# Prompt attention: V and the probabilities turned by VectorE in 32x32 squares, and a head's output row joined to the next head's scores

## The chip, the cores and the metric

The kernel runs on one core of one Trainium2 chip. TensorE does the matrix products, VectorE (DVE in the profile), ScalarE (ACT) and GpSimd (POOL) the rest of the arithmetic, and SyncE (SP) issues most transfers. The metric is the device time of one execution in microseconds (us); the median of several runs counts.

## The reference

One layer of a decoder trunk, for a prompt of 256 positions and for 8 sample sequences of 4 new positions that share the weights. All 288 rows go through one combined input projection; from it come a gated short convolution (mixer A), a dilated sliding-window attention (mixer B) and two gates. Behind them stand two output products, a norm, a gated convolution FFN and a second norm. Everything is float32.

What is changed here lies in mixer B for the prompt. It has three head groups with window and dilation (128, 1), (512, 4), (2048, 16), four heads of dimension 128 in each:

```python
sc = jnp.einsum('nrbqhd,nrbkhd->nrbhqk', qb, kw).astype(jnp.float32) * ATT_SCALE - bias
sc = jnp.where(valid[None, None, :, None], sc, -jnp.inf)
m = jnp.max(sc, axis=-1, keepdims=True)
p = jnp.exp(sc - m)
den = jnp.sum(p, axis=-1, keepdims=True)
o = jnp.einsum('nrbhqk,nrbkhd->nrbqhd', p / den, vw.astype(jnp.float32))
lse = jnp.swapaxes((m + jnp.log(den))[..., 0], 3, 4)
...
wg = jax.nn.softmax(jnp.stack(lses), axis=0)
yb = jnp.einsum('gnth,gnthd->nthd', wg, jnp.stack(outs)).reshape(n, t, ATT_OUT).astype(x.dtype)
```

Head j of the three groups is merged with weights that follow the softmax denominators. That equals one softmax over the keys of all three groups together, and the kernel computes it so: for one head j, one row of scores over group 0's keys and groups 1 and 2's keys of the same residue class, one exponential, one sum, one product with V.

## The kernel before

**Products.** Activations are kept transposed: features on the 128 partitions, 288 tokens along the columns. Each weight block (128 output features by up to 2048 input features) is loaded by SyncE into one of three buffers `wst` and split in two float32r parts, a half block of eight 128x128 tiles at a time: ScalarE rounds it to `whi`, VectorE subtracts to get `wlo` (`split`, L232). There are four buffers for each part. `mms` (L226, L227, L228) then issues three matmuls per tile (high x high, high weight x low activation, low weight x high activation), so a product of 16 tiles is 48 matmuls into one of six PSUM buffers `acc`. A half block can be refilled once TensorE has finished with what was in its buffers four half blocks before.

**Stages.** Queries of all heads come first. Then for each of the four heads j there are six products: K and V of the three groups. Behind these begins the attention of the prompt for head j, `prompt_attention`. It is a generator, which `prompt_step` moves on by one step behind each following product, so that its instructions fall into the next head's products (for the last head, into the products of the convolution stage that follows). A second, independent chain of steps (`sample_steps`) treats the sample group meanwhile: it multiplies tiles of the cache on ScalarE and VectorE (L478, L483) and reduces them with a transposing reduction on VectorE (L485).

**The order of the work.** A tile scheduler decides the order of each engine's instructions from the recorded program. What is held by hand: `behind(i, before)` orders one instruction behind another on its engine, and `in_a_row` does so for a list. A row of small matmuls is put behind the last matmul of a product (`last_mm`), so a row stands whole between two products.

**The attention of one head, before.** (1) GpSimd copies K and V of groups 1 and 2 into four classes by position (`k_cls`, `v_cls`, L379). (2) The scores' row on TensorE: two matmuls for group 0 (L384), and 32 of 32 rows each for the classes (L391), into two PSUM buffers `att`. (3) VectorE adds the distance penalties (L398, L404) and takes the maximum (L407, L408), ScalarE the exponential with its sum (L409), VectorE divides (L410, L411). Two blocks of 128 queries have 192 and 384 columns of probabilities. (4) Two products later a second row: six transposes of V (L418) and five of the probabilities (L423), 128x128 each, by TensorE against the identity. ScalarE copies the results out of PSUM in four instructions (L420 and L427). (5) One product later the third row, the output: six matmuls (L431, L432, L435), which sum V times probabilities over both kinds of keys, into another `att` buffer. ScalarE copies it to `oT` in token order (L441), and a split into `ybh`, `ybl` follows.

Of the kernel before, what the change touches and what calls it, by code (L numbers as in the profile page):

```python
# [18 lines left out]
P = 128  # L19
D = 2048  # L20
KD = D // P
SEQ = 256
NB, NT = 8, 4
NS = NB * NT
T = SEQ + NS
# [11 lines left out]
NG, NH = 3, 4  # L37
# [10 lines left out]
NM = NG * P  # L48
NC = 4
# [30 lines left out]
SQ = 32  # L80
# [18 lines left out]
def layer_kernel(ctx: ExitStack, tc: tile.TileContext, ins, outs):  # L99
    nc = tc.nc  # L100
    pe, dve, act, pool, sp = nc.tensor, nc.vector, nc.scalar, nc.gpsimd, nc.sync
# [4 lines left out]
    ps = ctx.enter_context(tc.tile_pool(name="ps", bufs=6, space=PSUM))  # L106
# [3 lines left out]
    def nm(s):  # L110
        uid[0] += 1
        return f"{s}_{uid[0]}"

    def sb(pl, shape, tag, dt=F32, bufs=None):
        return pl.tile(shape, dt, tag=tag, name=nm(tag), bufs=bufs)
# [4 lines left out]
    def h2(ap):  # L120
        return ap.rearrange("p (h a) -> p h a", h=2)

    def h3(ap):
        return ap.rearrange("p k (h a) -> p k h a", h=2)
# [5 lines left out]
    def att(cols=512):  # L130
        return sb(ps, [P, cols], "att", bufs=2)

    def f32(ap):
        return ap.bitcast(F32)
# [9 lines left out]
    def behind(i, after):  # L144

        tc.add_manual_dep(i.ins, after.ins.name, no_sync, reason="pace")
# [7 lines left out]
    w_split = []  # L154
# [40 lines left out]
    last_mm = [None]  # L195
# [35 lines left out]
    def split(hi, lo, src):  # L231
        return act.copy(hi, src), dve.tensor_tensor(lo, src, f32(hi), ALU.subtract)  # L232
# [29 lines left out]
    def first_w(lo, b, k0, n):  # L262
        k, h = slice(k0, k0 + n), slice(k0 % HK, k0 % HK + n)
        if b < 2:
            return (two_lo if lo else two_hi)[:, b, k]
        if b < 4 and not (lo and b == 3):
            return one[2 if lo else b - 2][:, k]
        return half[0 if b == 3 else 1 + lo][k0 // HK][:, h]

    raw, sp_row = [], []  # L270
    for n, (k0, nk) in enumerate(FIRST):
        k = slice(k0, k0 + nk)
# [4 lines left out]
    for n, (k0, nk) in enumerate(FIRST):  # L277
        k = slice(k0, k0 + nk)
        x_k = xs[:, k].rearrange("p k (a h) -> p k h a", h=2)
        act_row.append(act.copy(xh[:, k, :, :H], x_k))  # L280
        for b in range(1, N_FIRST):
            if b == 1:
                out, src = two_hi[:, :, k], raw[n][:, :2]
            else:
                out, src = first_w(False, b, k0, nk), raw[n][:, b]
# [33 lines left out]
    pa = sb(big, [P, KD * T], "yal")  # L319

    m_dist = [pa[:, :NM], pa[:, NM : 3 * NM]]
    v_cls = pa[:, 3 * NM : 3 * NM + 2 * 2 * P].rearrange("p (c k) -> p c k", c=NC)
    q_0 = pa[:, 3 * NM + 4 * P : 3 * NM + 6 * P].rearrange("p (b k) -> p b k", b=2)
    k_cls = pa[:, 3 * NM + 6 * P : 3 * NM + 10 * P].rearrange("p (c k) -> p c k", c=NC)
    pa_at = [3 * NM + 10 * P]

    def pa_take(n):
        pa_at[0] += n
        return pa[:, pa_at[0] - n : pa_at[0]]

    v = pa_take(2 * NG * P).rearrange("p (b d) -> p b d", d=P)
    s_two = [pa_take((b + 2) * P) for b in range(2)]
    xs_flat = xs.rearrange("p k t -> p (k t)")
    q_all = xs_flat[:, : NH * NG * T].rearrange("p (j g t) -> p j g t", j=NH, g=NG)
    sT_two = [xs_flat[:, NH * NG * T + 2 * b * P : NH * NG * T + (5 * b + 2 * (1 - b)) * P] for b in range(2)]
    sT_old = xs_flat[:, NH * NG * T : NH * NG * T + 4 * P].rearrange("p (b k) -> p b k", b=2)[:, :, :P]
    sT_cls = xs_flat[:, NH * NG * T : NH * NG * T + 6 * P].rearrange("p (b k) -> p b k", b=2)[:, :, P : 2 * P]
    oT = pa_take(2 * P)
    prm = sb(big, [P, R_W], "prm")
    ident = cst[:, C_ID : C_ID + P]  # L340

    ybh = sb(big, [P, NH, T], "ybh", F32R)
    ybl = sb(big, [P, NH, T], "ybl", F32R)
# [23 lines left out]
    def in_a_row(row):  # L367

        for before, i in zip(row, row[1:]):
            behind(i, before)  # L370

    def prompt_attention(j, qT, kT, vT):


        q5 = h3(qT)[:, :, :, :P].rearrange("p g r (b u c) -> p g b r c u", b=2, c=2)
        k_b, v_b = (t.rearrange("p c (b g u) -> p g c b u", b=2, g=2) for t in (k_cls, v_cls))
        for dst, src in ((k_b, kT), (v_b, vT)):
            for g in range(1, NG):
                pool.tensor_copy(dst[:, g - 1], src[:, g, :SEQ].rearrange("p (b u c) -> p c b u", b=2, c=NC))  # L379
        s3 = [att((b + 1) * P + (b + 1) * 2 * SQ) for b in range(2)]  # L380
        row = [last_mm[0]]
        for b in range(2):
            n = (b + 1) * P
            row.append(pe.matmul(s3[b][:, :n], q_0[:, b], kT[:, 0, :n], start=True, stop=True))  # L384
        for b in range(2):
            by_class = s3[b][:, (b + 1) * P :].rearrange("p (b g u) -> p g b u", g=2, u=SQ)
            for g in range(1, NG):
                for r in range(2):
                    for c in range(2):
                        at = slice(SQ * (2 * r + c), SQ * (2 * r + c + 1))  # L390
                        row.append(pe.matmul(  # L391
                            by_class[at, g - 1], q5[:, g, b, r, c], k_b[:, g - 1, 2 * c + r, : b + 1], start=True, stop=True
                        ))
        in_a_row(row)
        s = [s_two[b][:, : (b + 1) * (P + 2 * SQ)] for b in range(2)]
        for b in range(2):
            n = (b + 1) * P
            dve.scalar_tensor_tensor(  # L398
                s[b][:, :n], m_dist[b][:, :n], -SLOPE[0][j] / SCALE, s3[b][:, :n], ALU.mult, ALU.add
            )  # L400
            dst, src = (t[:, n:].rearrange("p (b g u) -> p g b u", g=2, u=SQ) for t in (s[b], s3[b]))
            for g in range(1, NG):
                m = m_dist[b][:, g * n : (g + 1) * n].rearrange("p (b u c) -> p b u c", u=SQ, c=NC)[:, :, :, 0]
                dve.scalar_tensor_tensor(dst[:, g - 1], m, -SLOPE[g][j] / SCALE, src[:, g - 1], ALU.mult, ALU.add)  # L404
        for b in range(2):
            st = sb(wk, [P, 4], "st", bufs=4)
            dve.reduce_max(st[:, 0:1], s[b], AX.X)  # L407
            dve.tensor_scalar_mul(st[:, 1:2], st[:, 0:1], -SCALE)  # L408
            act.activation(s[b], s[b], AF.Exp, bias=st[:, 1:2], scale=SCALE, accum_out=st[:, 2:3])  # L409
            dve.reciprocal(st[:, 3:4], st[:, 2:3])  # L410
            dve.tensor_scalar_mul(s[b], s[b], st[:, 3:4])  # L411
        yield 2
        pv = [att(NG * P) for _ in range(2)]
        row = [last_mm[0]]
        for n in range(2 * NG):
            out = pv[n // NG][:, n % NG * P : (n % NG + 1) * P]
            src = vT[:, 0, n * P : (n + 1) * P] if n < 2 else v_cls[:, n - 2]
            row.append(pe.transpose(out, src, ident))  # L418
        for n in range(2):
            act.copy(v[:, n * NG : (n + 1) * NG], pv[n].rearrange("p (b d) -> p b d", d=P))  # L420
        pt = [sb(ps, [P, (b + 2) * P], "acc") for b in range(2)]
        in_a_row(row + [
            pe.transpose(pt[b][:, c * P : (c + 1) * P], s_two[b][:, c * P : (c + 1) * P], ident)  # L423
            for b in range(2) for c in range(b + 2)
        ])
        for sT, t in zip(sT_two, pt):
            act.copy(sT, t)  # L427
        yield 1
        po = att(2 * P)
        row = [last_mm[0]]  # L430
        row.append(pe.matmul(h2(po), v[:, 0], sT_old, start=True, stop=False))  # L431
        row.append(pe.matmul(po[:, P:], v[:, 1], sT_two[1][:, P : 2 * P], start=False, stop=False))  # L432
        for c in range(NC):
            at = slice(c * SQ, (c + 1) * SQ)
            row.append(pe.matmul(  # L435
                h2(po)[:, :, at], v[:, 2 + 2 * (c % 2) + c // 2], sT_cls[:, :, at], start=False, stop=c == NC - 1
            ))
        in_a_row(row)
        o_b = oT.rearrange("p (r b u c) -> p b r c u", r=2, b=2, c=2)
        for b in range(2):  # L440
            act.copy(o_b[:, b], po[:, b * P : (b + 1) * P].rearrange("p (r c u) -> p r c u", r=2, c=2))  # L441
        split(h2(ybh[:, j])[:, :, :P], h2(ybl[:, j])[:, :, :P], oT.rearrange("p (h a) -> p h a", h=2))

    bmask = cst[:, C_BM : C_BM + MASK]

# [179 lines left out]
    for j in range(NH):  # L627
        kT, vT = (kv[:, j % 2, c] for c in range(2))
# [58 lines left out]
    for i in range(KD):  # L687
        ph = product(x)
        h = sb(wk, [P, T], "h", bufs=2)
        act.copy(h2(h), ph)  # L690
        pc = product(x)
        u = sb(wk, [P, UW + 2], "u", bufs=2)
# [216 lines left out]
    for part, nf in enumerate(THIRDS):  # L909
        gh = sb(big, [P, KD, T], "yah", F32R)  # L910
        gl = sb(big, [P, KD, T], "yal", F32R)
        for k in range(nf):
            pa = product(x_gb if part == 0 else x)
            u = sb(wk, [P, UW + 2], "u", bufs=2)
            up, us = conv_in(u[:, :UW], R_SF + f * 2 * NB)
            if part == 0:
                pa, b1 = normed(pa)
# [230 lines left out]
```

## Time and profile before

| What | Value |
|---|---|
| Median of 3 runs | 1723.63 us (1723.46 to 1723.65) |
| Profiled execution, its own time | 1723.19 us |
| Its span (first to last instruction) | 1721.4 us |
| Granted TensorE clock, mean | 0.998 |
| TensorE busy | 1709.2 us, 99% of the span |
| VectorE, ScalarE, GpSimd busy | 1122.3 (65%), 879.1 (51%), 275.0 us (16%) |
| Scores' rows of the four heads begin at | 115.19, 154.58, 193.98, 233.38 us |
| Rows of transposes begin at | 128.29, 167.70, 207.09, 246.50 us |
| Output rows begin at | 135.38, 174.78, 214.18, 253.59 us |

A matmul's duration in the profile is the time from its start to its modelled end. Matmuls overlap, so the time that one takes from TensorE is read from the starts of neighbours. A time in square brackets behind an instruction of another engine is the idle time just before it, with what ended it. All four heads lie between 70 and 260 us of the span; after that stage the kernel's work is not touched by the change.

### The profile page before, as it was taken

The numbers are of one execution on the slowest core, as the hardware profiler recorded it, in microseconds if no ns is written. First come the engines' busy times: TensorE is split into PE (matmuls) and PEld (weight loads), VectorE is DVE, ScalarE is ACT, GpSimd is POOL, SyncE is SP. The second block draws the span as 40 slices with busy tenths as digits, with TensorE's granted clock in tenths as the row PEclk, the third lists the DMA queues.
The fourth block names the chain that finished last, engine by engine and source line by source line (L and its number), as shares of the span: only waits on it lengthen the run. The fifth ranks groups of instructions, "written<-read, shape, count | busy, mean of one in ns | idle before, by whom it ended". The sixth has DMA issues, their size and how long they took to land.

```text
span 1721.4 us, 33808 instructions
## 1 busy us (share of the span) xinstructions
PE 1709.2 (99%) x14132; PEld 1703.5 (99%) x14132; DVE 1122.3 (65%) x1448; ACT 879.1 (51%) x1432; POOL 275.0 (16%) x431
## 2 busy tenths in 40 slices
PE   9999999999999999999999999999999999999997
PEld 9999999999999999999999999999999999999997
DVE  6457677775777765455788878855556554555575
ACT  5446555554555554444545655543455543344455
POOL 0011110000000000001454323300111100011165
PEclk9999999999999999999999999999999999999999
DMA  8766666665767776688876666667766766766662
GB/s 293 289 259 250 236 222 248 238 243 204 263 245 252 294 289 245 245 306 302 301 258 253 245 253 257 249 247 262 275 247 258 254 245 257 281 245 254 244 219 108
DMA packets 60824, 436.17 MB, mean 253 GB/s; under 512 B 7744, under 2 KB 13632, under 8 KB 21056
## 3 DMA queue, kind: packets, MB, share of 16 engines
q1 hardware_dynamic: 59376, 430.33, 68.0%
q10 hardware_dynamic: 1296, 3.69, 0.6%
q8 instruction: 110, 1.80, 0.4%
q14 instruction: 42, 0.34, 0.1%
HBM read 427.53 MB, written 94.53 MB: 303 GB/s over the span
## 4 chain that ended last, share of the span: by engine, by line
PE 99%; DMA 0%; DVE 0%; ACT 0%; SPq 0%; issue 0%; ACTq 0%; DVEq 0%
PE acc L226 32%; PE acc L227 32%; PE acc L228 32%; PE acc L311 2%; DMA wst<-in_w_in 0%; PE att L514 0%; DVE dd L861 0%; PE att L435 0%; PE att L418 0%; PE att L384 0%; PE acc L423 0%; ACT yah L868 0%; PE att L391 0%; PE att L544 0%; PE att L431 0%; DVE yah L859 0%
## 5 line engine op out<-in xcount | busy, mean ns | idle before, releaser
L232 DVE TENSOR_TENSOR wlo<-wst,whi 128x1024 fp32r<-128x1024 f32 (+1 forms) x574 | 703.1, 1225 | 464.5 <-ACT whi L232 460.5
L232 ACT CAST whi<-wst 128x1024 fp32r<-128x1024 f32 (+1 forms) x574 | 586.2, 1022 | 761.4 <-PE acc L227 688.9
L226 PE MATMUL acc<-xh,whi 128*128 128x288 f32 (+1 forms) x3184 | 909.2, 286 | 0.0
L227 PE MATMUL acc<-xl,whi 128*128 128x288 f32 (+1 forms) x3184 | 907.7, 285 | 0.0
L228 PE MATMUL acc<-xh,wlo 128*128 128x288 f32 (+1 forms) x3184 | 907.6, 285 | 0.0
L226 PEld LDWEIGHTS acc<-xh,whi 128*128 128x128 f32 x3184 | 599.1, 188 | 1.4 <-issue 0.8
L228 PEld LDWEIGHTS acc<-xh,wlo 128*128 128x128 f32 x3184 | 599.1, 188 | 0.0
L227 PEld LDWEIGHTS acc<-xl,whi 128*128 128x128 f32 x3184 | 599.0, 188 | 0.0
L228 PE MATMUL acc<-yah,wlo 128*128 128x288 f32 x1216 | 347.7, 286 | 0.0
L227 PE MATMUL acc<-yal,whi 128*128 128x288 f32 x1216 | 347.7, 286 | 0.0
L226 PE MATMUL acc<-yah,whi 128*128 128x288 f32 x1216 | 347.6, 286 | 0.0
L228 PEld LDWEIGHTS acc<-yah,wlo 128*128 128x128 f32 x1216 | 229.8, 189 | 0.0
L227 PEld LDWEIGHTS acc<-yal,whi 128*128 128x128 f32 x1216 | 229.8, 189 | 0.0
L226 PEld LDWEIGHTS acc<-yah,whi 128*128 128x128 f32 x1216 | 229.7, 189 | 0.0
L668 POOL COPY qk_s<-u 128x2 f32<-128x2 f32 x44 | 36.4, 828 | 562.7 <-ACT u L922 441.6
L485 DVE TRANSPOSE_TENSOR_REDUCE sw<-cache 128x32 f32<-128x1024 f32 x64 | 79.7, 1245 | 5.2 <-ACT cache L478 1.1
L656 DVE SCALAR_TENSOR_TENSOR cy<-u,prm,cy 128x304 f32<-128x304 f32 x120 | 70.7, 589 | 3.5 <-ACT cy L654 0.7
L727 POOL TENSOR_TENSOR ya<-ya,dd 128x288 f32<-128x288 f32 x16 | 13.8, 859 | 294.4 <-DVE ya L726 288.8
L478 ACT ACTIVATE cache<-cache,qk_s 128x128 f32<-128x128 f32 x128 | 43.2, 392 | 0.0
L232 ACT CAST yah<-ya 128x288 fp32r<-128x288 f32 x76 | 32.5, 428 | 20.5 <-POOL ya L727 8.2
L478 ACT ACTIVATE cache<-cache,dd 128x128 f32<-128x128 f32 x128 | 42.1, 390 | 0.0
L679 DVE TENSOR_TENSOR ya<-cy,acc 128x256 f32<-128x256 f32 x88 | 23.3, 304 | 25.6 <-PE acc L228 25.6
(219 smaller groups left out, 1015.4 us busy)
## 6 DMA issues: line engine op xcount, KB each, us to landing
wst<-in_w_in SPq DMA_DIRECT2D x111, 1024.0 KB, 4.9
wst<-in_w_up SPq DMA_DIRECT2D x88, 1024.0 KB, 4.9
wst<-in_w_down SPq DMA_DIRECT2D x32, 1024.0 KB, 4.9
cache<-in_ck SPq DMA_DIRECT2D x18, 1024.0 KB, 6.5
cache<-in_cv SPq DMA_DIRECT2D x18, 1024.0 KB, 6.2
wst<-in_w_a SPq DMA_DIRECT2D x16, 1024.0 KB, 4.9
wst<-in_w_out SPq DMA_DIRECT2D x16, 1024.0 KB, 5.3
wst<-in_w_down SPq DMA_DIRECT2D x16, 768.0 KB, 4.4
```

The source lines that it names most:

```text
L226: pe.matmul(out, hi[:, c, :], xh_k, start=k == 0, stop=False)
L227: pe.matmul(out, hi[:, c, :], xl_k, start=False, stop=False)
L228: last_mm[0] = pe.matmul(out, lo[:, c, :], xh_k, start=False, stop=k == nk - 1)
L232: return act.copy(hi, src), dve.tensor_tensor(lo, src, f32(hi), ALU.subtract)
L311: i = pe.matmul(o[b], first_w(term == 2, b, k, 1)[:, 0], xk, start=k == 0 and term == 0, stop=k == KD - 1 and term == 2)
L478: i = act.activation(e_t, e_t, AF.Copy, scale=w[:, g + 1, j, b * NT + t : b * NT + t + 1])
L485: dve.tensor_reduce(parts[:, g, :, j, b * NT : (b + 1) * NT].rearrange("p k j t -> p j t k"), c[:, 2 * half * cols : (2 * half + 2) * cols ...
L656: dve.scalar_tensor_tensor(y, u[:, i : i + YW], prm[:, w0 + i : w0 + i + 1], y, ALU.mult, ALU.add)
L668: pool.tensor_copy(dst[:, 0:2], u[:, SEQ : SEQ + 2])
L679: dve.tensor_tensor(a, b, c, ALU.mult)
L727: pool.tensor_tensor(m, m, ma[:, i], ALU.add)
```

## The change

Steps (1) to (3) stay. Step (4) leaves TensorE:

- VectorE turns V and the probabilities in 32x32 squares, each square in its place: V of group 0 (256 columns) from `vT` into a new buffer `v_sq`; V's classes (512 columns, which GpSimd now writes into `v_sq`) in place; and all five blocks of probabilities (640 columns, now in one buffer `s_blk`) in place.
- A turned square of rows 32i and columns 32k still has to go to rows 32k and columns 32i. That is done by copies of one pair (i, k) for all blocks at once: 16 copies of 32 partitions by 6 x 32 for V, on ScalarE, into `v`; 16 copies of 32 partitions by 5 x 32 for the probabilities, on VectorE, into `sT_blk`. They are issued in parts: five of V's in the first step behind the scores, then with each of three products four (the last time three) of V's and six (the last time four) of the probabilities', and each is ordered behind the last weight split of its engine.

Step (5) is a function `output`, kept in `pending`: for heads 0 to 2 its six matmuls become the first part of the next head's scores' row, six products after the head's own scores. Its PSUM buffer is one of `acc` instead of `att`. For the last head the output row stands alone, six products after that head's scores, in the convolution stage.

```diff
-    v_cls = pa[:, 3 * NM : 3 * NM + 2 * 2 * P].rearrange("p (c k) -> p c k", c=NC)
...
+    v, v_sq, q_0, k_cls = (pa_blocks(n) for n in (2 * NG, 2 * NG, 2, NC))
+    v_cls = v_sq[:, 2:]
+    s_blk = pa_blocks(5)
+    s_two = [s_blk[:, 2 * b : 2 + 3 * b].rearrange("p b k -> p (b k)") for b in range(2)]
...
+    sT_blk = xs_flat[:, NH * NG * T : NH * NG * T + 5 * P].rearrange("p (b k) -> p b k", b=5)
...
+    pending = []
+
+    def output(j):
+
+        po = sb(ps, [P, 2 * P], "acc")
+        row = [pe.matmul(h2(po), v[:, 0], sT_old, start=True, stop=False)]
+        row.append(pe.matmul(po[:, P:], v[:, 1], sT_blk[:, 3], start=False, stop=False))
+        for c in range(NC):
+            at = slice(c * SQ, (c + 1) * SQ)
+            row.append(pe.matmul(
+                h2(po)[:, :, at], v[:, 2 + 2 * (c % 2) + c // 2], sT_cls[:, :, at], start=False, stop=c == NC - 1
+            ))
...
+        return row
+
     def prompt_attention(j, qT, kT, vT):
...
-        row = [last_mm[0]]
+        row = [last_mm[0]] + (pending.pop()() if pending else [])
...
-        yield 2
-        pv = [att(NG * P) for _ in range(2)]
-        row = [last_mm[0]]
-        for n in range(2 * NG):
-            out = pv[n // NG][:, n % NG * P : (n % NG + 1) * P]
-            src = vT[:, 0, n * P : (n + 1) * P] if n < 2 else v_cls[:, n - 2]
-            row.append(pe.transpose(out, src, ident))
-        for n in range(2):
-            act.copy(v[:, n * NG : (n + 1) * NG], pv[n].rearrange("p (b d) -> p b d", d=P))
-        pt = [sb(ps, [P, (b + 2) * P], "acc") for b in range(2)]
-        in_a_row(row + [
-            pe.transpose(pt[b][:, c * P : (c + 1) * P], s_two[b][:, c * P : (c + 1) * P], ident)
-            for b in range(2) for c in range(b + 2)
-        ])
-        for sT, t in zip(sT_two, pt):
-            act.copy(sT, t)
         yield 1
...
+        dve.transpose(v_sq[:, :2].rearrange("p b k -> p (b k)"), vT[:, 0, :SEQ])
+        v_c = v_cls.rearrange("p c k -> p (c k)")
+        dve.transpose(v_c, v_c)
+        s_all = s_blk.rearrange("p b k -> p (b k)")
+        v_moves, s_moves = ([(n, (n + r) % 4) for r in range(4) for n in range(4)] for _ in range(2))
+
+        def move(eng, dst, src, n, split_n):
+            for _ in range(n):
+                if moves[dst is v]:
+                    i, k = moves[dst is v].pop()
+                    at, to = slice(i * SQ, (i + 1) * SQ), slice(k * SQ, (k + 1) * SQ)
+                    behind((act.copy if eng is act else dve.tensor_copy)(dst[to, :, at], src[at, :, to]), w_split[split_n])
+
+        moves = s_moves, v_moves
+        move(act, v, v_sq, 5, 0)
+        yield 1
+        dve.transpose(s_all, s_all)
+        for n in range(3):
+            move(act, v, v_sq, 4, 0)
+            move(dve, sT_blk, s_blk, 6, 1)
+            yield 1
+        pending.append(partial(output, j))
+        if j == NH - 1:
+            yield 1
+            in_a_row([last_mm[0]] + pending.pop()())
```

In the changed program TensorE's instructions stand in the same order as before but for these rows, and SyncE's queue is the same instruction for instruction. On GpSimd only the order of a few copies for a head's first queries and classes changes.

More of the change, by code (lines that the diff above doesn't have):

```diff
@@ L321, in layer_kernel @@
     m_dist = [pa[:, :NM], pa[:, NM : 3 * NM]]
-    v_cls = pa[:, 3 * NM : 3 * NM + 2 * 2 * P].rearrange("p (c k) -> p c k", c=NC)
-    q_0 = pa[:, 3 * NM + 4 * P : 3 * NM + 6 * P].rearrange("p (b k) -> p b k", b=2)
-    k_cls = pa[:, 3 * NM + 6 * P : 3 * NM + 10 * P].rearrange("p (c k) -> p c k", c=NC)
-    pa_at = [3 * NM + 10 * P]
+    pa_at = [3 * NM]
     def pa_take(n):
@@ L329, in pa_take, with pa_blocks @@
         return pa[:, pa_at[0] - n : pa_at[0]]
-    v = pa_take(2 * NG * P).rearrange("p (b d) -> p b d", d=P)
-    s_two = [pa_take((b + 2) * P) for b in range(2)]
+    def pa_blocks(n):
+        return pa_take(n * P).rearrange("p (b k) -> p b k", b=n)
+    v, v_sq, q_0, k_cls = (pa_blocks(n) for n in (2 * NG, 2 * NG, 2, NC))
+    v_cls = v_sq[:, 2:]
+    s_blk = pa_blocks(5)
+    s_two = [s_blk[:, 2 * b : 2 + 3 * b].rearrange("p b k -> p (b k)") for b in range(2)]
     xs_flat = xs.rearrange("p k t -> p (k t)")
     q_all = xs_flat[:, : NH * NG * T].rearrange("p (j g t) -> p j g t", j=NH, g=NG)
-    sT_two = [xs_flat[:, NH * NG * T + 2 * b * P : NH * NG * T + (5 * b + 2 * (1 - b)) * P] for b in range(2)]
+    sT_blk = xs_flat[:, NH * NG * T : NH * NG * T + 5 * P].rearrange("p (b k) -> p b k", b=5)
     sT_old = xs_flat[:, NH * NG * T : NH * NG * T + 4 * P].rearrange("p (b k) -> p b k", b=2)[:, :, :P]
@@ L370, in in_a_row @@
             behind(i, before)
+    pending = []
[8 more added lines that the diff above has]
+            ))
+        o_b = oT.rearrange("p (r b u c) -> p b r c u", r=2, b=2, c=2)
+        for b in range(2):
+            act.copy(o_b[:, b], po[:, b * P : (b + 1) * P].rearrange("p (r c u) -> p r c u", r=2, c=2))
+        split(h2(ybh[:, j])[:, :, :P], h2(ybl[:, j])[:, :, :P], oT.rearrange("p (h a) -> p h a", h=2))
+        return row
     def prompt_attention(j, qT, kT, vT):
@@ L421, in prompt_attention @@
-        pt = [sb(ps, [P, (b + 2) * P], "acc") for b in range(2)]
-        in_a_row(row + [
-            pe.transpose(pt[b][:, c * P : (c + 1) * P], s_two[b][:, c * P : (c + 1) * P], ident)
-            for b in range(2) for c in range(b + 2)
-        ])
-        for sT, t in zip(sT_two, pt):
-            act.copy(sT, t)
-        yield 1
[L429 to L442, printed above, removed]
+        yield 1
```

## The prediction

> **What bounds the kernel now.** I read the page first: its first part (busy time) and fourth part (the chain that ended last), then TensorE's own list of waits, because a chain that is all TensorE can still hide starved stretches.
>
> ```profile
> PE 1709.2 (99%) x14132; PEld 1703.5 (99%) x14132; DVE 1122.3 (65%) x1448; ACT 879.1 (51%) x1432; POOL 275.0 (16%) x431
> ...
> PE 99%; DMA 0%; DVE 0%; ACT 0%; SPq 0%; issue 0%; ACTq 0%; DVEq 0%
> ```
> ```profile
> PE acc L311 <- ACT yal L289: 1.6, 2, 1.1
> PE acc L244 <- DVE cy L241: 1.2, 1, 1.2
> PE acc L841 <- DVE dd L861: 0.3, 1, 0.3
> PE acc L846 <- DVE h L833: 0.3, 1, 0.3
> ```
>
> Columns of the second view: who waits, for whom; total us, times, longest. These are all of TensorE's waits: start and end of the kernel, none in the attention stage. So an instruction taken off TensorE's queue between about 115 and 255 us shortens the kernel by its pitch (start to next start), not by its duration, as long as TensorE's inputs stay early. The prediction has two halves: how much pitch goes, and whether the inputs stay early.
>
> **What leaves TensorE: the transposes.** Each head has a row of 11 (six for V, L418; five for the probabilities, L423) between two products. First and last head in the timeline (start us, busy us, then the instruction and its count):
>
> ```profile
> 128.17 0.28 PE L228 MATMUL acc<-xh,wlo 128*128 128x288 f32 x1
> 128.29 0.38 PE L418 MATMUL att<-cst,dd 128*128 128x128 f32 x2
> 128.51 0.60 PE L418 MATMUL att<-cst,yal 128*128 128x128 f32 x4
> 128.95 0.71 PE L423 MATMUL acc<-cst,yal 128*128 128x128 f32 x5
> 129.41 0.37 PE L226 MATMUL acc<-xh,whi 128*128 128x288 f32 x1
> 129.62 0.29 PE L227 MATMUL acc<-xl,whi 128*128 128x288 f32 x1
> ...
> 246.50 0.38 PE L418 MATMUL att<-cst,dd 128*128 128x128 f32 x2
> ...
> 247.62 0.37 PE L226 MATMUL acc<-xh,whi 128*128 128x288 f32 x1
> 247.82 0.29 PE L227 MATMUL acc<-xl,whi 128*128 128x288 f32 x1
> ```
>
> Product matmuls start 0.12 us apart (128.17, 128.29). From the first transpose to the second product matmul behind the row is 129.62 - 128.29 = 1.33 us; one product pitch of 0.12 would be there anyway, so the row costs 1.21 us, of which 0.09 is the seam: the first product matmul behind it starts 0.21 before its successor instead of 0.12. The last head gives 1.32 - 0.12 = 1.20. Four heads: 4 x 1.205 = 4.82 us. Without transposes the seam goes too, so all of it counts.
>
> Within the row, 129.41 - 128.29 = 1.12 us for 11 is 0.10 us per transpose, although one alone lasts about 0.27 (two overlapped take 0.38, less one spacing). The Trainium skill, TensorE: Matmul & The Clock Gate, Part 4, gives about 275 ns for a transpose inside a kernel. That is this trace's duration, not its spacing; counted by it the sum would be 44 x 0.275 = 12.1 us by estimate, and this is a rival below.
>
> **What moves on TensorE: the output row.** It keeps its six matmuls per head, but for heads 0 to 2 stands directly ahead of the next head's scores:
>
> ```profile
> 135.38 0.59 PE L431 MATMUL att<-yah,yal 128*128 128x256 f32 x2
> ...
> 136.84 0.37 PE L226 MATMUL acc<-xh,whi 128*128 128x288 f32 x1
> 137.05 0.29 PE L227 MATMUL acc<-xl,whi 128*128 128x288 f32 x1
> ...
> 154.58 0.82 PE L384 MATMUL att<-dd,yal 128*128 128x128 f32 x4
> 155.32 0.56 PE L391 MATMUL att<-yal,yah 128*32 128x32 f32 x32
> 155.82 0.39 PE L226 MATMUL acc<-xh,whi 128*128 128x288 f32 x1
> 156.04 0.29 PE L227 MATMUL acc<-xl,whi 128*128 128x288 f32 x1
> ```
>
> The row takes 1.46 us and has the same exit seam, 0.21 - 0.12 = 0.09. Joined, three of these go: at most 0.27. The new joint between output and scores isn't in this trace; a change of shape inside a row costs something of the order of the exit seam, so the gain lies between 0 and 0.27. I take 0.2, nearer the measured seam. **Sum on TensorE:** 4.82 + 0.2 = 5.0 us.
>
> **What the other engines get.** Per head VectorE gains three square transposes over 256, 512 and 640 columns, and 16 copies of 32 partitions by 5 x 32 for the probabilities. ScalarE gains 16 copies of 32 by 6 x 32 for V, and loses the four evacuations of the transposes. GpSimd and SyncE keep their instructions; no DMA is added or moved in its queue. These rows bound the prices (the first is a line's own statistics, min/median/max ns):
>
> ```profile
> L287 DVE CAST cache<-wst x2: 222/224/226, 5.1 to 6.7; 128x128 fp32r<-128x128 f32 x2
> ```
> ```profile
> 155.73 0.29 DVE L398 SCALAR_TENSOR_TENSOR yal<-yal,att 128x128 f32<-128x128 f32 x1 [1.71 <-PE att L391]
> 155.93 0.32 DVE L404 SCALAR_TENSOR_TENSOR yal<-yal,att 128x32 f32<-128x32 f32 x2
> 156.18 1.21 DVE L232 TENSOR_TENSOR wlo<-wst,whi 128x1024 fp32r<-128x1024 f32 x1
> 157.31 0.75 DVE L483 TENSOR_TENSOR cache<-cache,qk_s 128x512 f32<-128x512 f32 x1
> 157.98 0.41 DVE L398 SCALAR_TENSOR_TENSOR yal<-yal,att 128x256 f32<-128x256 f32 x1
> 158.31 0.43 DVE L404 SCALAR_TENSOR_TENSOR yal<-yal,att 128x64 f32<-128x64 f32 x2
> ...
> 158.93 1.23 DVE L485 TRANSPOSE_TENSOR_REDUCE sw<-cache 128x32 f32<-128x1024 f32 x1
> 160.09 0.50 DVE L407 TENSOR_REDUCE st<-yal 128x1 f32<-128x384 f32 x1
> ...
> 161.95 0.32 DVE L411 TENSOR_SCALAR yal<-yal,st 128x192 f32<-128x192 f32 x1
> ```
> ```profile
> 170.20 0.84 ACT L420 COPY yal<-att 128x384 f32<-128x384 f32 x2
> 170.93 0.76 ACT L427 COPY yah<-acc 128x256 f32<-128x256 f32 x2
> ```
>
> A copy of 160 columns lies between the cast of 128 columns (0.22) and the scaling of 192 (0.32). I take 0.28; 16 make 4.5 us. Bounds: 0.12 (half the pair of 32-column instructions at 155.93, overlapped) and 0.75 (512 columns). The square transpose has its nearest row in the transposing reduction: 1.23 us for 1024 columns, pro rata 0.31, 0.61 and 0.77 for 256, 512 and 640. With a little fixed time each I take 0.4, 0.7 and 0.8, 1.9 per head; bounds 1.7 (pro rata) and 3.7 (1.23 each). VectorE: +6.4 us per head. ScalarE: 16 copies of 192 columns at 0.3 to 0.38 (the 256-column copy) are about 5.1 us, less 0.84 + 0.76: +3.5 us.
>
> All of this I cost at nothing, and the cover is the lead of the weight split. Each half block of weights is rounded by ScalarE (whi) and subtracted by VectorE (wlo) ahead of its product:
>
> ```profile
> 182.29 1.04 ACT L232 CAST whi<-wst 128x1024 fp32r<-128x1024 f32 x1 [1.90 <-PE acc L227]
> 185.23 1.05 ACT L232 CAST whi<-wst 128x1024 fp32r<-128x1024 f32 x1 [0.42 <-PE acc L227]
> ```
> ```profile
> 183.37 1.22 DVE L232 TENSOR_TENSOR wlo<-wst,whi 128x1024 fp32r<-128x1024 f32 x1 [1.72 <-ACT whi L232]
> ```
>
> TensorE frees a half block every 185.23 - 182.29 = 2.94 us; with four buffers it comes to the refilled one three half blocks later, 8.8 us after the release. The split is done 183.37 + 1.22 - 182.29 = 2.3 us after it: 6.5 us to spare. The whole gain hangs on whether the attention work eats these 6.5 us.
>
> ```profile
> 154.60:178.20 23.60, 23.60 (x221) 23.12 (x220) 17.39 (x28) 15.32 (x34) 3.90 (x5) 1.00 0.58 217
> ```
>
> This stretch (columns: length; busy of PE, PEld, DVE, ACT, POOL; granted clock, DMA share, GB/s) is the four products behind head 1's scores, where the new work falls. VectorE is busy 17.39 of 23.6 us; with 6.4 more it is full. So I walk its queue in the changed program's order, times from the start of the joined row:
>
> Scores end at 1.46 + 1.15 = 2.6 (155.73 - 154.58 = 1.15). Six bias additions, a transposing reduction, the earlier head's split and a maximum reach 5.6; V's transpose to 6.3; the rest of the statistics and one wlo to 8.1. ScalarE meanwhile does V's first five copies, which wait for that transpose, and stand ahead of both exponentials: these end at 9.5 and the next whi at 10.6, released at 8.7. VectorE scales, turns the probabilities (10.9), then wlo (12.1), a cache product, six copies, a reduction, and the wlo that ends at 16.8: TensorE needs it at 20.4, 3.6 to spare. The wlo behind the second six copies ends at 22.6 against 26.3, 3.7 to spare; behind the last four and the next head's first transpose, 26.3 against 32.2, 5.9 to spare. Then the queue drains (the next product's stretch is light). So the lead falls to 3.6 us and TensorE doesn't wait. Head 3 has two convolution additions in the stretch, and I find about 4 us there.
>
> Other waits. V's transpose waits for GpSimd's class copies:
>
> ```profile
> 157.46 1.11 POOL L379 COPY yal<-dd 128x256 f32<-128x256 f32 x1
> ```
>
> This ends 158.57 - 154.58 = 4.0 us into the row; VectorE comes to it at 5.6. The output row needs the last copies: they are issued two products ahead of it (over 10 us). Loads of raw weights follow the late wlo by its lateness, at most 3 to 4 us; a load is due 2.5 products (14.7 us) after the release that the wlo before it followed, which needs 2.3 us, the lateness and the landing:
>
> ```profile
> wst<-in_w_in SPq DMA_DIRECT2D x111, 1024.0 KB, 4.9
> ```
>
> That leaves 14.7 - 2.3 - 4.9 = 7.5, above the lateness.
>
> **Against which time.** The profiled execution took 1723.19 us (span 1721.4 and 1.8 around it), 0.44 below the median 1723.63. Less 5.0: 1718.2, or 1718.6 on the median's basis. I predict 1718.5.
>
> **Rivals.** *VectorE starves TensorE (slower).* Place: the first products behind each head's scores. With 16 copies at x us instead of 0.28, the spares above are used up at 0.28 + 3.7/12 = 0.59. A head then loses 16 (x - 0.59), and the gain of 1.25 per head is gone at x = 0.67. At 0.75, the 512-column row, each loses 2.6: 1718.5 + 10.2 = 1728.7. For it: VectorE has no reserve there, and every copy moves to other partitions. Against: five times fewer columns per copy would have to cost as much as 512.
> The pair of 32-column instructions at 155.93 overlaps (0.32 for two). The Trainium skill, VectorE: DVE Perf Modes, section Two Vector instructions with no wait between them, says that an instruction whose 32-partition quadrant differs from the one before is held until that has finished; the 16 copies alternate quadrants, so by it they don't overlap. By estimate that keeps them at 0.28 or more apart, which the walk assumes; no run here shows it yet.
>
> *Late in places.* One or two heads, most likely head 3, wait 1 to 4 us: 1719.5 to 1722.5. For it: a lead of under 4 us by a hand walk. Against: it is still a whole half block.
>
> *The saving counts by duration.* 44 x 0.27 = 11.9 us: 1711.7. Against it, the row of 11 begins and ends within 1.33 us.
>
> *No change.* Something else ends at the same time, 1723.6. Against: the chain and TensorE's empty wait list.
>
> **How the numbers follow.** Forecast 0.84 (own range 1717.6 to 1719.4: seam 0 to 0.27, the two bases, and some tenths); late in places 0.05; starved 0.06; by duration 0.02; no change 0.03. The range 1717.4 to 1720.4 holds the forecast and the milder part of the late case, some 0.86. A change of this kernel under 0.2% (3.4 us) can't be told from none. Faster: 0.84 + 0.02 + 0.03 of the late case = 0.89; same: 0.02 + 0.03 = 0.05; slower 0.06.
>
> **What would show it.** Right: no TensorE transposes until the sample group's own; the output row directly ahead of the next scores and about 2.7 us with them; TensorE's waits still empty in 115 to 275 us; ScalarE's and VectorE's small copies near 0.3 us each; wlo instructions up to 4 us later against their products. Wrong: idle time of TensorE put down to wlo (VectorE) or whi (ScalarE) there, copies above 0.55 us, or a square transpose well above a microsecond.

## The result and the profile after

| | Before | After |
|---|---|---|
| Median of 9 runs each, us | 1723.52 (1723.27 to 1723.95) | 1718.73 (1718.47 to 1719.67) |
| Profiled execution, us | 1723.19 | 1718.68 |
| Its span, us | 1721.4 | 1716.9 |
| Granted TensorE clock, mean | 0.998 | 0.999 |
| TensorE busy, us | 1709.2 | 1705.5 |
| VectorE, ScalarE busy, us | 1122.3, 879.1 | 1143.8, 895.4 |

The kernel is faster: the ratio after to before is 0.9972, with an interval of 0.9964 to 0.9981. The medians differ by 4.79 us.

The page of the changed kernel, its busy times and its chain; then the list of all that TensorE waits for:

```profile
PE 1705.5 (99%) x14088; PEld 1700.3 (99%) x14088; DVE 1143.8 (67%) x1524; ACT 895.4 (52%) x1480; POOL 280.3 (16%) x431
...
PE 99%; DVE 0%; ACT 0%; DMA 0%; ACTq 0%; issue 0%; DVEq 0%
```
```profile
PE acc L244 <- DVE cy L241: 1.2, 1, 1.2
PE acc L311 <- ACT yal L289: 0.9, 1, 0.9
PE acc L854 <- DVE dd L874: 0.3, 1, 0.3
PE acc L859 <- DVE h L846: 0.3, 1, 0.3
```

44 matmuls are gone (14132 to 14088), VectorE has 21.5 us and ScalarE 16.3 us more work, and the chain is TensorE's as before. The list of waits has no `wlo` and no `whi`: in the attention stage TensorE still waits for nothing.

TensorE's timeline (start us, busy us, then the instruction and its count) shows where the scores of head 0 begin, and the row of head 1 as it is now, the output of head 0 (from L379 on) and then the scores (from L404 on):

```profile
115.56 0.82 PE L404 MATMUL att<-dd,yal 128*128 128x128 f32 x4
...
152.21 0.59 PE L379 MATMUL acc<-yah,yal 128*128 128x256 f32 x2
...
153.70 0.87 PE L404 MATMUL att<-dd,yal 128*128 128x128 f32 x4
...
155.00 0.39 PE L226 MATMUL acc<-xh,whi 128*128 128x288 f32 x1
155.22 0.29 PE L227 MATMUL acc<-xl,whi 128*128 128x288 f32 x1
```

From the row's start to the second product matmul behind it is 155.22 - 152.21 = 3.01 us. Nothing is left of the row of transposes. To the first product matmul the joined row takes 155.00 - 152.21 = 2.79 us; the two rows before, read to the same point, take 1.46 + 1.24 = 2.70, which is the 2.7 that were forecast; the 0.09 more is the seam, which comes back at the joint (see the experiments). The span is 4.5 us shorter rather than 4.8 because head 0's scores begin 0.37 us later than before (115.56 against 115.19), ahead of all that the change touches.

What the change does in its stage can be read free of that: from head 0's first score to the first matmul of the sample group's own row behind the stage. These are its lines, before and after:

```profile
372.90 0.25 PE L535 MATMUL att<-qk_s 128*32 128x32 f32 x5
```
```profile
368.52 0.22 PE L548 MATMUL att<-qk_s 128*32 128x32 f32 x2
```

The stretch takes 372.90 - 115.19 = 257.71 us before and 368.52 - 115.56 = 252.96 us after, so 4.75 us less. It is called the stage below, and in one trace against another it shows differences that the spread of the medians hides.

The new instructions, each as the statistics of its line (min/median/max ns, from when to when):

```profile
L433 DVE STREAM_TRANSPOSE yal<-dd x4: 390/404/433, 93.3 to 216.6; 128x256 f32<-128x256 f32 x4
L435 DVE STREAM_TRANSPOSE yal<-yal x4: 665/696/701, 121.1 to 234.4; 128x512 f32<-128x512 f32 x4
L449 DVE STREAM_TRANSPOSE yal<-yal x4: 845/846/846, 128.4 to 239.2; 128x640 f32<-128x640 f32 x4
L444 ACT COPY yal<-yal x64: 347/349/353, 121.8 to 252.3; 32x192 f32<-32x192 f32 x64
L444 DVE COPY yah<-yal x64: 245/250/625, 130.3 to 254.2; 32x160 f32<-32x160 f32 x64
```

The three square transposes were taken at 0.4, 0.7 and 0.8 us, and have 0.404, 0.696 and 0.846. The copies of 160 columns were taken at 0.28 us and have 0.250.

VectorE's queue in head 1, the stretch that the prediction walked by hand (start us, busy us, line, count):

```profile
165.43 1.57 DVE L444 COPY yah<-yal 32x160 f32<-32x160 f32 x6
167.03 1.25 DVE L498 TRANSPOSE_TENSOR_REDUCE sw<-cache 128x32 f32<-128x1024 f32 x1
168.20 2.32 DVE L232 TENSOR_TENSOR wlo<-wst,whi 128x1024 fp32r<-128x1024 f32 x2
...
171.15 1.57 DVE L444 COPY yah<-yal 32x160 f32<-32x160 f32 x6
...
173.92 2.32 DVE L232 TENSOR_TENSOR wlo<-wst,whi 128x1024 fp32r<-128x1024 f32 x2
```

Six copies take 1.57 us and the last of them 0.25, so they start 0.264 apart, a little more than one lasts. A `wlo` takes about 1.18 us here. The first one behind the first six copies so ends at 169.38, which is 17.2 us after the row's start (16.8 in the prediction), and the first behind the second six at 175.10, 22.9 us after it (22.6).

### The profile page after: what moved, and what is told of

It reads as the page before. It is cut to its first block, busy times and chain, and to the rows that moved or that the text cites. A ratio compares the mean times of both kernels' runs of the same rounds, so it can differ in the third digit from the quotient of the medians.

```text
span 1716.9 us, 33841 instructions
## 1 busy us (share of the span) xinstructions
PE 1705.5 (99%) x14088; PEld 1700.3 (99%) x14088; DVE 1143.8 (67%) x1524; ACT 895.4 (52%) x1480; POOL 280.3 (16%) x431
## 4 chain that ended last, share of the span: by engine, by line
PE 99%; DVE 0%; ACT 0%; DMA 0%; ACTq 0%; issue 0%; DVEq 0%
PE acc L226 32%; PE acc L227 32%; PE acc L228 32%; PE acc L311 2%; DMA wst<-in_w_in 0%; PE att L527 0%; DVE dd L874 0%; PE acc L383 0%; PE att L404 0%; ACT yah L881 0%; PE att L411 0%; PE att L557 0%; PE acc L379 0%; DVE yah L872 0%; PE att L784 0%; PE acc L380 0%
## 5 line engine op out<-in xcount | busy, mean ns | idle before, releaser
L232 ACT CAST yah<-ya 128x288 fp32r<-128x288 f32 x76 | 32.5, 428 | 20.3 <-DVE ya L697 8.1
```

## The experiments

The theory under test (A): TensorE is the bound, the transposes cost it their spacing, and the new work of VectorE and ScalarE is hidden by the lead of the weight split. The rivals: the saving goes by the transposes' duration; the join carries a part of the gain; the new work costs something that the waits don't show (E in the expectations). All runs that follow are set against runs of the kernel before on the same chip: median 1723.85 us (18 runs) for the joined row, the squares, the doubled transposes and the copies three times; 1723.96 us (17 runs) for the others.

### The joined row without the squares

The kernel before, with its transposes on TensorE; only the output row is joined to the next head's scores. The diff leaves out the function `output`, which is that of the change.

```diff
...
-        row = [last_mm[0]]
+        row = [last_mm[0]] + (pending.pop()() if pending else [])
...
+        pending.append(partial(output, j))
+        if j == NH - 1:
+            yield 3
+            in_a_row([last_mm[0]] + pending.pop()())
```

> The kernel before with one part of the change: the output row joins the next head's scores (last head: alone), the 44 transposes stay on TensorE. Theory A (the joint costs as much as the seam it saves, read from the rows of the trace after): 1723.5 us, joined rows of 3.01 us to the second product matmul. Prediction's term (0.2 us saved, at most 0.27): 1723.3 us. Rival B (the joining carries the gain, the transposes were hidden): 1718.7 us.

Measured: 1723.68 us (1723.04 to 1724.43), ratio 1.0000 (0.9991 to 1.0009). Its timeline, TensorE, head 1's joined row:

```profile
153.21 0.59 PE L377 MATMUL acc<-yah,yal 128*128 128x256 f32 x2
...
154.70 0.87 PE L402 MATMUL att<-dd,yal 128*128 128x128 f32 x4
...
156.00 0.39 PE L226 MATMUL acc<-xh,whi 128*128 128x288 f32 x1
156.22 0.29 PE L227 MATMUL acc<-xl,whi 128*128 128x288 f32 x1
```

It is again 156.22 - 153.21 = 3.01 us long. The median moves by nothing that can be measured, but its interval is wide enough to hide the 0.2 us that were forecast. The stage is sharper: 373.06 - 115.36 = 257.70 us, against 257.71 before. Joining alone brings nothing.

### The squares without the joined row

The changed kernel, but each head's output row stands alone, a product ahead of the next head's scores.

```diff
-        pending.append(partial(output, j))
-        if j == NH - 1:
-            yield 1
-            in_a_row([last_mm[0]] + pending.pop()())
+        in_a_row([last_mm[0]] + output(j))
...
-        row = [last_mm[0]] + (pending.pop()() if pending else [])
+        row = [last_mm[0]]
```

> The changed kernel with the output row standing alone one product ahead of the next scores: the squares without the joining. Theory A (all of the gain is the pitch of the 44 transposes, 4 x 1.20 us): 1718.7 us. Prediction's terms: 1718.9 us. Rival B (the joining carries the gain): 1723.5 us. A wait of TensorE for the last copies of V or of the probabilities, which now have one product less of time, would add up to a few us and stand in TensorE's waits at the output row.

Measured: 1718.54 us (1718.32 to 1718.93), ratio 0.9969 (0.9956 to 0.9981): the whole gain, without the join. Its stage takes 368.37 - 115.48 = 252.89 us, 4.82 less than before. Its timeline, TensorE, the output row of head 0 and the scores' row of head 1:

```profile
146.24 0.59 PE L379 MATMUL acc<-yah,yal 128*128 128x256 f32 x2
...
147.71 0.37 PE L226 MATMUL acc<-xh,whi 128*128 128x288 f32 x1
147.91 0.29 PE L227 MATMUL acc<-xl,whi 128*128 128x288 f32 x1
...
153.67 0.82 PE L404 MATMUL att<-dd,yal 128*128 128x128 f32 x4
...
155.14 0.29 PE L227 MATMUL acc<-xl,whi 128*128 128x288 f32 x1
```

The output row takes 147.91 - 146.24 = 1.67 us and the scores 155.14 - 153.67 = 1.47. Put together, one product pitch of 0.12 is counted twice: 1.67 + 1.47 - 0.12 = 3.02 us, which is the length of the joined row. The seam that joining removes (147.91 - 147.71 - 0.12 = 0.08 us) comes back at the joint. In the joined row the output takes 153.70 - 152.21 = 1.49 us to the first score, against 1.47 to the first product when it stands alone, and the scores take 155.22 - 153.70 = 1.52 us against 1.47.

### Each transpose twice

The kernel before, with every transpose on TensorE issued twice.

```diff
-            row.append(pe.transpose(out, src, ident))
+            row += [pe.transpose(out, src, ident) for _ in range(2)]
...
-            for b in range(2) for c in range(b + 2)
+            for b in range(2) for c in range(b + 2) for _ in range(2)
```

> The kernel before with each of its 44 transposes issued twice into the same place; nothing else. Theory A (a transpose costs its pitch, 0.109 us): 44 x 0.109 = 4.8 us more, 1728.3 us. Rival (it costs its duration, 0.27 us): 12 us more, 1735.5 us. Rival (transposes are hidden): 1723.5 us.

Measured: 1728.38 us (1727.97 to 1729.02), ratio 1.0027 (1.0016 to 1.0038), so 4.5 us more for 44 transposes more. Its timeline, TensorE, the row of head 0:

```profile
128.22 0.60 PE L418 MATMUL att<-cst,dd 128*128 128x128 f32 x4
128.65 1.04 PE L418 MATMUL att<-cst,yal 128*128 128x128 f32 x8
129.53 1.25 PE L423 MATMUL acc<-cst,yal 128*128 128x128 f32 x10
130.54 0.37 PE L226 MATMUL acc<-xh,whi 128*128 128x288 f32 x1
130.74 0.29 PE L227 MATMUL acc<-xl,whi 128*128 128x288 f32 x1
```

The row goes from 128.22 to the second product matmul at 130.74: 2.52 us instead of 1.33, so 1.2 us for 11 transposes, or 0.109 each. The stage is 377.61 - 115.11 = 262.50 us long, 4.79 more than before. By duration it would have been 44 x 0.27 = 12 us more. That rival falls: a transpose costs TensorE its spacing.

### The new work taken away

The changed kernel, with three whole copies on VectorE in place of the three square transposes and the 32 small copies of each head. V and the probabilities reach the output row unturned: the turning is left out of the computation.

```diff
-        dve.transpose(v_sq[:, :2].rearrange("p b k -> p (b k)"), vT[:, 0, :SEQ])
-        dve.transpose(v_c, v_c)
...
-        move(act, v, v_sq, 5, 0)
+        behind(dve.tensor_copy(v[:, :2], vT[:, 0, :SEQ].rearrange("p (b k) -> p b k", b=2)), w_split[1])
+        behind(dve.tensor_copy(v[:, 2:], v_cls), w_split[1])
         yield 1
-        dve.transpose(s_all, s_all)
-        for n in range(3):
-            move(act, v, v_sq, 4, 0)
-            move(dve, sT_blk, s_blk, 6, 1)
-            yield 1
+        behind(dve.tensor_copy(sT_blk, s_blk), w_split[1])
+        yield 3
```

> The changed kernel without the turning: three whole-tile copies by VectorE (256, 512 and 640 columns) in place of the three square transposes and the 32 small copies per head, so V and the probabilities reach the output row unturned (that part of the computation is left out). Theory A (the new work on VectorE and ScalarE is wholly hidden): 1718.7 us, as the changed kernel. Rival E (the small copies cost TensorE something, by shared memory or by late splits): below, 1716 to 1718 us.

Measured: 1719.09 us (1718.44 to 1719.54), ratio 0.9971 (0.9961 to 0.9982). The same stretch of head 1 in both kernels, by windows (columns: length; busy of PE, PEld, DVE, ACT, POOL with counts; granted clock, DMA share, GB/s), the changed kernel and then this one:

```profile
152.20:190.40 38.20, 38.20 (x338) 37.72 (x337) 33.12 (x56) 27.57 (x61) 6.06 (x8) 1.00 0.71 271
```
```profile
152.20:190.40 38.20, 38.20 (x338) 37.72 (x338) 27.95 (x40) 22.09 (x45) 5.86 (x8) 1.00 0.65 240
```

VectorE and ScalarE each have over 5 us less to do, TensorE does the same 338 matmuls in the same time, and the kernel is no faster; its stage takes 368.96 - 116.01 = 252.95 us, as in the changed kernel. So the turning costs the changed kernel nothing, and the gain is all that the transposes' time on TensorE is worth.

### How far the cover reaches: VectorE's copies twice and three times

The changed kernel, with each small copy of VectorE issued two or three times.

```diff
-                    behind((act.copy if eng is act else dve.tensor_copy)(dst[to, :, at], src[at, :, to]), w_split[split_n])
+                    for _ in range(1 if eng is act else 2):
+                        behind((act.copy if eng is act else dve.tensor_copy)(dst[to, :, at], src[at, :, to]), w_split[split_n])
```

(3 in place of 2 in the second kernel.)

> The changed kernel with each of VectorE's 64 small copies made twice: 4.2 us more of VectorE's time per head (16 x 0.26). Theory A (hidden up to the spare, 2.9 us for head 0, 3.6 to 5 for the others): head 0 loses about 1 us, the others next to nothing: 1719.5 us (1718.7 to 1721.5). A loss in proportion to the time added, from threefold copies (19.9 us for 33 us): 1728.7 us.

> The changed kernel with each of VectorE's 64 small copies made three times in a row: 8 us more of VectorE's time per head (32 x 0.25), same output. Theory A (hidden up to the spare of the weight split, at its least 2.9 us for head 0 and 3.6 to 5 for the others in the trace after; what exceeds it starves TensorE): about 5 + 4 + 2 + 3 us more, 1733 us (1723 to 1742), with TensorE idle and put down to wlo. Rival C (VectorE's work in this stage is hidden at any size so far): 1718.7 us. Rival D (VectorE's time counts in full): 1718.7 + 32 = 1751 us.

Measured: twice 1723.19 us (1722.84 to 1724.12), ratio 0.9997 (0.9987 to 1.0006); three times 1738.59 us (1738.19 to 1738.81), ratio 1.0084 (1.0071 to 1.0098). The waits of TensorE that are new, of the kernel with two and the kernel with three (total us, times, longest):

```profile
PE acc L228 <- DVE wlo L232: 3.0, 4, 1.3
```
```profile
PE acc L228 <- DVE wlo L232: 13.3, 13, 3.5
```

This is the wait on `wlo` that the rival of the starved TensorE named, though later: with two copies it comes 25 us behind the scores of head 0 and then 31 to 32 us behind those of heads 0, 2 and 3, in the fifth and sixth product, and head 1 has none. With two copies a loss of about 1 us was expected. The gain that is left is 1723.96 - 1723.19 = 0.8 of 4.8 us, so the loss is 4.0, and the stage agrees (372.37 - 115.41 = 256.96 us, 4.00 more than in the changed kernel). The idle time alone is 3.0 of it. The rest lies at the ends of the waits: at the first, three neighbouring matmuls start at 140.41, 141.60 and 141.83, so 1.42 us stand where two spacings of 0.12 would, with an idle time of 0.91. Each wait so costs some 0.27 us beyond its idle time, and 3.0 + 4 x 0.27 = 4.1. VectorE's queue in head 0, first of the changed kernel, then with two copies, shows the first of the four waits:

```profile
130.34 1.57 DVE L444 COPY yah<-yal 32x160 f32<-32x160 f32 x6
...
133.79 1.57 DVE L444 COPY yah<-yal 32x160 f32<-32x160 f32 x6
...
136.56 2.79 DVE L232 TENSOR_TENSOR wlo<-wst,whi 128x1024 fp32r<-128x1024 f32 x2
```
```profile
130.19 3.34 DVE L445 COPY yah<-yal 32x160 f32<-32x160 f32 x12
...
135.42 2.17 DVE L445 COPY yah<-yal 32x160 f32<-32x160 f32 x6
...
138.91 1.38 DVE L445 COPY yah<-yal 32x160 f32<-32x160 f32 x5
140.32 1.23 DVE L232 TENSOR_TENSOR wlo<-wst,whi 128x1024 fp32r<-128x1024 f32 x1
```

In the changed kernel 12 copies, 3.14 us, stand ahead of the `wlo` that ends at 137.75 (the first of the pair at 136.56); TensorE uses it at 140.68, so 2.9 us are to spare. With two copies it is 23 copies and 3.34 + 2.17 + 1.38 = 6.89 us: 3.75 more. Eleven copies at the spacing of 0.264 would be 2.9, just the spare. But in this kernel the copies start some 0.28 apart (twelve in 3.34 us), and one in the group at 135.42 was slow (it takes 2.17 us for six, where 1.66 would do); that is 0.9 us more, and makes the wait. So the cover is thinner in head 0 than the 3.6 to 4 us that the prediction found in heads 1 and 3. The other three waits lie at 147.8, 225.7 and 264.6 us; ahead of the first of them stand eight copies, a reduction and the next head's first transpose without a `wlo` between, so there the order that the scheduler chose may have a part in it.

With three copies, where 1733 us (1723 to 1742) were expected, the kernel is 14.7 us slower than before, and its stage is 388.65 - 115.50 = 273.15 us long, 20.2 more than in the changed kernel. The waits of 13.3 us and 13 x 0.27 = 3.5 us at their ends don't explain all of it. TensorE's timeline behind the longest wait (in square brackets the idle time before the instruction and what ended it), and the windows around it (columns as above):

```profile
225.52 0.28 PE L227 MATMUL acc<-xl,whi 128*128 128x288 f32 x1
229.28 0.47 PE L228 MATMUL acc<-xh,wlo 128*128 128x288 f32 x1 [3.47 <-DVE wlo L232]
229.54 0.45 PE L226 MATMUL acc<-xh,whi 128*128 128x288 f32 x1
...
232.89 0.29 PE L228 MATMUL acc<-xh,wlo 128*128 128x288 f32 x1
233.02 0.28 PE L226 MATMUL acc<-xh,whi 128*128 128x288 f32 x1
```
```profile
225.00:229.20 4.20, 0.81 (x7) 0.59 (x5) 3.99 (x7) 1.34 (x2) 0.69 (x1) 1.00 0.40 168
229.20:233.00 3.80, 3.72 (x16) 3.72 (x17) 3.55 (x10) 0.00 (x0) 0.00 (x0) 0.55 0.00 0
233.00:236.00 3.00, 3.00 (x27) 3.00 (x26) 2.81 (x9) 1.05 (x1) 0.00 (x0) 1.00 0.91 306
```

After 3.47 us of idleness the matmuls start 0.24 us apart instead of 0.12, for 3.6 us, and the granted clock of that stretch is 0.55. So this wait is paid one and a half times: 3.5 us of idleness and some 1.8 us of half speed behind it (15 matmuls by 0.12). A second stretch of that kind, at 280.7, adds some 1.5 us (13 matmuls by 0.12), and with both the sum is 20.1 of the 20.2 us. The Trainium skill, TensorE: Matmul & The Clock Gate, Part 1, says that TensorE falls to half its clock after an idle window of about 3.4 us and comes back after as long a busy one; this wait and the 3.6 us behind it agree.

### ScalarE's copies three times

The same edit on the other engine: `for _ in range(3 if eng is act else 1)`.

> The changed kernel with each of ScalarE's 64 small copies made three times: 11.5 us more of ScalarE's time per head (32 x 0.36), which with the 26 to 28 us that it is busy per 38 us leaves it no idle time. Theory A (the same spare covers ScalarE, since rounding and subtracting are one chain): 11.5 less about 4 per head are lost, and some more where TensorE's clock drops behind long waits: 1745 us (1725 to 1755), put down to whi and wlo. Rival F (ScalarE's work isn't on that chain's edge): 1718.7 us.

Measured: 1734.53 us (1734.25 to 1734.67), ratio 1.0062 (1.0048 to 1.0076), less of a loss than the 1745 expected, and inside the range of 1725 to 1755. TensorE's new waits:

```profile
PE acc L228 <- DVE wlo L232: 7.7, 11, 0.7
PE acc L226 <- ACT whi L232: 3.3, 6, 0.6
```

More of them are put down to VectorE, although only ScalarE has more to do: the subtraction of a half block waits for ScalarE's rounding, so both come late together, and six waits are on the rounding itself. None is longer than 0.7 us, and none has a stretch of half clock behind it, which the expectation had reckoned with. The stage is 384.22 - 115.59 = 268.63 us long, 15.7 more than in the changed kernel; 11.0 us of idle time and 17 x 0.27 = 4.6 at the ends of the waits make 15.6. ScalarE's share of the cover is limited too: at three times its small copies the kernel is 10.6 us slower than before.

## Why the prediction was right

**The transposes: right, and the whole of the gain.** 4.82 us were forecast from the starts of neighbours. Each transpose twice gave 4.79 us more in its stage and 4.5 in its median; the squares alone brought 4.82 in the stage and 1723.85 - 1718.54 = 5.3 by medians of runs that spread over 1.3 and 0.6 us; the change itself brought 4.75 in the stage and 4.79 by its median.

**The joined row: the one term that was wrong.** 0.2 us were taken out of 0 to 0.27, "nearer the measured seam". By the rows of the traces it is 0.00, and joining alone leaves the stage as it was: the joint costs what the seam costs. The lower bound was the true value; the choice between the bounds was made without a row of such a joint. The sum of 5.0 was too large by this 0.2. The median is 0.23 above the forecast of 1718.5, which is less than its runs spread.

**The cover: right in head 1, missed in head 0.** The walk of VectorE's queue gave 3.6, 3.7 and 5.9 us to spare in head 1; matched with TensorE's matmuls it is 3.6, 3.8 and 5.6. That it came out so close is in part luck. The three `wlo` end at 17.2, 22.9 and 26.9 us behind the row's start (16.8, 22.6 and 26.3 in the walk), so VectorE was later than walked, although a copy is spaced 0.264 us where 0.28 was taken. But TensorE needs them at 20.8, 26.7 and 32.5 us (20.4, 26.3 and 32.2), later by nearly as much. What the walk missed is head 0, where the spare is least, 2.9 us; the prediction had head 3 as the likeliest to be late. A likely reason is that in head 0 no output row of 1.5 us stands ahead of the scores, so that the products, and with them the need of `wlo`, come sooner against VectorE's work. The squares without the join have this in every head, and there the least spares of heads 1 to 3 are 1.9, 3.4 and 3.0 us, where the changed kernel has 3.6, 4.9 and 3.6. The order of VectorE's work differs too, so the reason isn't shown by itself.

**ScalarE: a little dearer.** Its copies last 0.349 us and are spaced 0.36, so 16 make 5.7 us, where about 5.1 were taken. Hidden all the same.

**The rivals.** *VectorE starves TensorE* had the right mechanism: with two copies per square 0.8 us of the gain are left, and with three the kernel is slower than before by 14.7 us. The point from which it decides was put too far out: the spares were to be used up at 0.59 us a copy and the gain to be gone at 0.67, but two copies of together 0.56 already cost 4.0 us. By the walk nothing should have been lost below 0.59; it had neither head 0's spare nor the slow copies nor the time at the ends of waits. *By duration* was excluded by the doubled transposes. *Late in places* didn't occur; *no change* fell with the result.

## What to carry to other kernels

On an engine that is the bound, a removed instruction is worth its spacing in its row, not its duration; joining rows of small matmuls brings nothing by itself when the joint costs as much as the seam that it removes, so a term of that kind needs a row of its own or is taken at nothing. Work that is moved to other engines is free up to the least spare of any place, not the spare of the place that looks fullest: follow the queue of each repetition, the first one too, and count on the scheduler not spreading the load evenly. Past that point a wait costs more than its idle time: some 0.27 us more each here, and behind two of the longest another 1.5 to 1.8 us, as the clock was at half.

## What the runs showed of the hardware

- **Small copies don't overlap on either engine.** VectorE's 32-partition copies are spaced 0.264 us at a duration of 0.250 (six in 1.57). This agrees with what the prediction cited from the Trainium skill, VectorE: DVE Perf Modes, section Two Vector instructions with no wait between them, that an instruction of another quadrant is held until the one before has finished. No run here puts two copies of the same quadrants behind each other, so that the quadrant is the cause isn't shown. ScalarE's small copies behave alike, five in 1.79 us at 0.349 each:

```profile
159.19 1.79 ACT L444 COPY yal<-yal 32x192 f32<-32x192 f32 x5
```

  That wasn't expected: in the kernel before its copies over all partitions ran into the next (those at 170.20 end at 171.04, and the next start at 170.93). The Trainium skill, ScalarE: Activation LUTs, section What ACT_TABLE_LOAD costs, says that ACTIVATE instructions behind each other overlap by about 93 ns; the large copies overlap by 0.11 us, close to that, the small ones not at all.

- **A copy on VectorE beside a copy on GpSimd takes two to three times as long.** The longest of the 64 copies, 0.625 us instead of 0.250, starts at 176.27, while GpSimd's class copy runs from 175.16, and ends at 176.90, 0.12 us after that one's end at 176.78:

```profile
175.16 1.62 POOL L399 COPY yal<-dd 128x256 f32<-128x256 f32 x1 [18.88 <-ACT dd L649]
```

  Over the three kernels with more copies 12 such copies took 0.48 to 0.77 us, each ending 0.11 to 0.12 us after the GpSimd copy. The Trainium skill, SBUF — State Buffer, section Who interferes with whom, describes this as an exclusive lock on a port pair that the two engines share, held for a whole instruction; the ends agree with it. No run here took the GpSimd copies away, so that cause is not shown by itself.
- **Half clock behind a shorter idle time.** In the kernel with three copies the matmuls also started 0.24 us apart from 280.8 to 283.9, where the wait just before, which ended at 279.5, was 1.9 us; waits of 1.5 and 1.6 us elsewhere had no such stretch behind them. By the page's rule above, an idle window of about 3.4 us, this one should have had none. The granted clock of this trace says more: it is at half from 229.46 to 232.87 us and from 280.66 to 284.07, so for 3.41 us both times, and the second begins 51.20 us, 15 such lengths, after the first. That looks as if the clock were decided at fixed moments 3.41 us apart. In the 3.41 us ahead of the second stretch TensorE was idle for 1.91, ahead of the first for 3.24; in no other from 115 to 290 us for more than 1.50. So a limit between 1.5 and 1.9 us of idle time in such a stretch fits; two cases don't prove it.
